# The second MLP product in three chunks: one group of 1024 output columns by seven products, in place of two groups of 512

## The chip, the cores and the metric

The kernel runs on one core of a Trainium2 chip. The metric is the device time of one launch in microseconds (us). TensorE (PE) multiplies into PSUM, which holds eight banks of 128 x 512 numbers; VectorE (DVE), ScalarE (ACT) and GpSimd (POOL) work on tiles; SyncE (SP) issues most DMAs. The engines run side by side, each through its own queue, and wait for one another by semaphores.

## The reference, cut to what matters

A decoder layer on 512 tokens of width 1024: two token mixers, a merge, and an MLP with a hidden width of 4096. The change is in the last product of the MLP.

```python
x = x + merged @ w_out[l]
h = rms_norm(x, norm_mlp[l])
x = x + jnp.square(jax.nn.relu(h @ w_ff1[l])) @ w_ff2[l]
return rms_norm(x, norm_final)
```

`h` is 512 x 1024, `w_ff1` 1024 x 4096, `w_ff2` 4096 x 1024, all float32.

## The kernel before, in words

**Precision.** A float32 operand is split into a high half (ACT copies it with rounding) and a low half (DVE subtracts: the line `DVE.tensor_tensor(l, t, h.bitcast(F32), op=ALU.subtract)`, L309). A product of two split operands is three matmuls: high by high, high by low, low by high. So each step of 128 in depth is three matmuls on PE, and every weight costs one ACT and one DVE instruction before PE can use it.

**The MLP** runs in four chunks `c` of 1024 hidden columns. In each, the first product gives the chunk's activations and the second adds their share to the output. Both are done by a scheme of seven products on 2 x 2 blocks in place of eight: the seven weight operands are three quarters of the weight block (A11, A12, A22) and four sums (S1 to S4), the seven activation operands are three blocks (y11, y21, y22) and four sums (yT1 to yT4). S1 = A21 + A22 and S3 = A11 + A21 are made in DRAM by DMAs (SP copies a quarter, POOL adds another, `make_sum` and `add_sum`); S2 = S3 + A22 and S4 = S2 + A12 are made in SBUF by DVE from weights that are there already (L318, and L297 where A12 is loaded a second time).

**The second product before the change** (`Out`, chunks 0 to 2) works in two groups `h` of 512 output columns. Each group's quarters of the weights are 512 rows by 256 columns. A product is 24 matmuls of 256 columns (L1520): the activations are stationary, the weights stream, two halves `f` of 128 tokens go to the two halves of one PSUM bank. Seven products in two groups are 14 x 24 = 336 matmuls per chunk. `OUT_TURN` gives the order; the first entry of a name is group 0, the second group 1. Three products add to a bank that an earlier one has left: A12 to A11's, S4 to S1's, A22 to S3's (`AFTER`). Before that the earlier product must have been **taken**: DVE adds the bank to the output `XX` (L1540, rows `x<-x,psB`) or, for A11 and S2, to a sum `U` that is kept through the chunks (L1536, rows `MA<-MA,psB`; in chunk 0 A11 is copied there by ACT, L1534). At the end `fold` adds `U` to three quarters of the output (L1546): group 1 after chunk 2, group 0 after chunk 3.

**Chunk 3** (`LAST`) does columns 0 to 511 by an `Out` of its own (`head`) and columns 512 to 1023 by plain matmuls of 512 columns (L395), in between.

**Weights.** Five buffers `raw` take loads from DRAM in the order of use; a buffer is loaded again as soon as its weights are split, or, where they go into a sum (`SUM_OF`), when that sum has been made (`give_back`). Three pairs of slots (`wh`/`wl` twice, `w3h`/`w3l`) hold the split weights; a slot is filled anew when PE has left the product that used it. In the orders below the pairs are `wh_4960`/`wl_4961`, `wh_4979`/`wl_4980` and `w3h`/`w3l`.

**What sets the order.** The program writes matmuls, and between them it lets the preparation of weights (`ahead`) and the side work (`step_side`: takes, activations, their sums and splits) go on by steps. A scheduler then orders each engine's instructions, and may put a later one ahead of one that it expects to wait. Each engine runs its queue in that order.

Of the kernel before, what the change touches and what calls it, by code (L numbers as in the profile page):

```python
# [13 lines left out]
F32 = mybir.dt.float32  # L14
FR = mybir.dt.float32r
AF = mybir.ActivationFunctionType
ALU = mybir.AluOpType
# [45 lines left out]
def trunk(ctx: ExitStack, tc: tile.TileContext, A, out):  # L63
    nc = tc.nc
    PE, ACT, DVE, POOL = nc.tensor, nc.scalar, nc.vector, nc.gpsimd
# [71 lines left out]
    LAST = 3  # L137
    FIRST = ("A11", "A12"), ("S1", "S3", "S2"), ("A22", "S4")
    IN_TURN = ("A11", "S3", "S1", "S2", "A12", "A22", "S4")
    OUT_TURN = ("A11", "A11", "S1", "S1", "A12", "A12", "S3", "S3", "A22", "A22", "S2", "S4", "S2", "S4")  # L140
    LAST_TURN = ("A11", "S1", "A12"), ("S3", "A22", "S2", "S4")
    dp = ctx.enter_context(tc.tile_pool(name="sums", bufs=1, space=bass.MemoryType.DRAM))
    jobs, late = [], []

    def quarters(layer, c, g):

        w, r, o = ((w_f1, 0, 1024 * c + 512 * g), (w_f2, 1024 * c, 512 * g))[layer - 1]
        return {f"{i + 1}{j + 1}": w[r + 512 * j:r + 512 * j + 512, o + 256 * i:o + 256 * i + 256].rearrange(
            "(k p) c -> p k c", p=128) for i in range(2) for j in range(2)}

    def add_group(layer, c, g):

        q = quarters(layer, c, g)
        of = {"A" + k: v for k, v in q.items()}
        final = layer == 2 and c == LAST
        for o in ("S1", "S3", "S2", "S4")[:4 if final else 4 - layer]:
            of[o] = dp.tile([128, 4, 256], F32, name=f"{o}_{layer}{c}{g}")
        jobs.append((of["S1"], q["21"], q["22"]))
        jobs.append((of["S3"], q["11"], q["21"]))
        if late:  # L160
            jobs.append(late.pop())
        if layer == 1:
            late.append((of["S2"], of["S1"], q["11"]))
        if final:
            jobs.append((of["S2"], of["S3"], q["22"]))
            jobs.append((of["S4"], of["S2"], q["12"]))
        return of
# [19 lines left out]
    for c in range(4):  # L187
# [7 lines left out]
        if c < LAST:  # L195
            of = [add_group(2, c, g) for g in range(2)]
            seen = {}
# [92 lines left out]
    def group_steps(i):  # L290

        key, at = WL[i]
        if i in PLUS:
            while st["load"] <= PLUS[i]:
                assert emit_load()
            t = raws.pop(PLUS[i])[0]
            DVE.tensor_tensor(t, t, held[key], op=ALU.add)  # L297
            give_back(held.pop(key))
            yield
        elif isinstance(at, str):  # L300
            t = held.pop(key)
        else:
            while st["load"] <= at:
                assert emit_load()
            t = raws.pop(at)[0]
        h, l = slot_of(i)
        ACT.activation(h, t, AF.Copy)  # L307
        yield
        DVE.tensor_tensor(l, t, h.bitcast(F32), op=ALU.subtract)  # L309
        hls[i] = tuple(x.rearrange("p (a b) -> p a b", a=4) for x in (h, l))  # L310
        to = SUM_OF.get(key)
        if to is None:
            give_back(t)
        elif to not in held:
            held[to] = t
        else:
            yield
            DVE.tensor_tensor(t, t, held[to], op=ALU.add)  # L318
            give_back(held[to])
            held[to] = t  # L320
# [62 lines left out]
    def use(key):  # L383
        i = st["use"]
        st["use"] += 1
        assert WL[i][0] == key, (WL[i][0], key)
        while st["prep"] <= i:
            emit_prep_half()
        return hls.pop(i)
# [21 lines left out]
    def step_side():  # L411
        for _ in range(len(side)):
            g = side.popleft()
            try:
                next(g)
                side.append(g)
            except StopIteration:
                pass
# [794 lines left out]
    def bank():  # L1213
        return ps3.tile([128, S], F32, tag="B", bufs=8, name="psB")
# [143 lines left out]
    def pair(f, i):  # L1358
        return f[:, 512 * i:512 * i + 512]
# [18 lines left out]
    def until(ready):  # L1378
        while not ready():
            assert side  # L1380
            step_side()

    class Group:
# [3 lines left out]
        def __init__(self, c, g, Y):  # L1387
            self.c, self.g, self.Y = c, g, Y
            self.s = pair(GBf, 6 + g)
            self.u2, self.u3, self.c21 = pair(MAf, 6 + g), pair(MAf, 0), pair(MAf, 1)  # L1390
            self.ps, self.done = {}, set()

        def pe(self, o):
            key = f"{o}1{self.c}{self.g}"
            until(lambda: o not in self.NEEDS or self.NEEDS[o] in self.done)
            if not self.done:
                side.append(self.main())
            name, x, *at = self.X[o]

            def mm(out, w, f, k, u, v, **kw):  # L1400
                PE.matmul(out, w[u][:, k, 128 * f:128 * f + 128], XB[x][v][:, k, :], **kw)  # L1401
            if not at:
                self.ps[name] = bank()
            product(self.ps[name], key, not at, mm)
            if at:
                side.append(self.last(name, *at))
            self.done.add(o)
# [95 lines left out]
    class Out:  # L1503
# [25 lines left out]

        def take(self, o, ps):  # L1530
            yield
            if o in ("A11", "S2"):
                if o == "A11" and self.c == 0:
                    ACT.activation(self.U, ps, AF.Copy)  # L1534
                else:
                    DVE.tensor_tensor(self.U, self.U, ps, op=ALU.add if o == "A11" else ALU.subtract)  # L1536
            else:
                i, j = {"A12": (0, 0), "S4": (0, 1), "A22": (1, 0)}.get(o, (1, 1))
                x = self.quarter(i, j)
                DVE.tensor_tensor(x, x, ps.rearrange("p (t c) -> p t c", t=2), op=ALU.subtract if i else ALU.add)  # L1540
            self.done.add(o)
# [6 lines left out]
                yield  # L1548
                yield

    def in_turn(groups, turn):

        seen = {}
        for o in turn:
            n = seen.get(o, 0)
            seen[o] = n + 1
            groups[n].pe(o)

    mode["pool"] = False
    for c in range(4):  # L1560
        Y = Hidden(c == LAST)
        gs = [Group(c, g, Y) for g in range(2)]
        if c == 0:
            for o in FIRST[0]:
                for g in gs:
                    g.pe(o)
            while not turned[0]:
                step_side()
            for os in FIRST[1:]:
                for g in gs:  # L1570
                    for o in os:
                        g.pe(o)
        else:
            for g in gs:
                for o in IN_TURN:
                    g.pe(o)
        if c < LAST:
            outs = [Out(c, h, Y) for h in range(2)]
            in_turn(outs, OUT_TURN)
            if c == LAST - 1:  # L1580
                side.append(outs[1].fold())

    def out_of(t):
        return MA[:, 2 * t:2 * t + 2, :].rearrange("p j c -> p (j c)")
# [22 lines left out]

    head = Out(LAST, 0, Y)
    keep([f"f2{LAST}1{i}" for i in range(4)], OT)
    in_turn([head], LAST_TURN[0])  # L1610
    w = []
    ps = [bank() for _ in range(2)]
    for i in range(4):
# [5 lines left out]
    for t in range(2):  # L1619
        add_x(t, 1, ps[t])  # L1620
        square_sum(t, 1)
    in_turn([head], LAST_TURN[1])
    gB = GBf[:, 0:D]
    nc.sync.dma_start(gB, bcast(A["norm_final"], D))
    while head.done != set(head.X):
# [48 lines left out]
```

## Time and profile before

| | us |
|---|---|
| median of 3 runs (812.71 to 813.44) | 813.04 |
| profiled execution, device time | 817.64 |
| its span | 815.9 |
| PE busy | 789.4 (97%) |
| DVE busy | 613.5 (75%) |
| ACT busy | 483.8 (59%) |
| POOL busy | 188.9 (23%) |
| second product, chunk 0, 1, 2 (first matmul to the next chunk's first) | 42.59, 41.12, 41.09 |
| first product, chunk 1, 2 | 39.94, 39.93 |

A row of the timeline gives the start, the duration, the engine, the line, what is written from what, the shapes, and in brackets how long the engine was idle before and what ended that. Matmuls overlap: the pace is the distance between starts, not the duration. Times within the span count from its start. L numbers are lines of the kernel before.

### The profile page before, as it was taken

What the parts mean: (1) busy time and instruction counts of PE and PEld (TensorE: products, weight loads), DVE (VectorE), ACT (ScalarE), POOL (GpSimd) and SP (SyncE); (2) the same over time, 40 slices, a digit from 0 to 9 for tenths busy, and PEclk for the clock granted to TensorE, in tenths of its full rate; (3) what the DMA queues carried; (4) which work ended last, traced back from release to release, by engine and by line L of the source; (5) the groups of instructions that cost most, each with busy time, mean ns of one, the idle gap of its engine ahead of it and who ended that gap; (6) DMA issues with size and microseconds to landing.
All of it is one profiled execution on the core that took longest, in us unless ns stands there. A gap on an engine that the chain in (4) does not pass through costs nothing.

```text
span 815.9 us, 14127 instructions
## 1 busy us (share of the span) xinstructions
PE 789.4 (97%) x5163; PEld 711.4 (87%) x5163; DVE 613.5 (75%) x1152; ACT 483.8 (59%) x957; POOL 188.9 (23%) x253
## 2 busy tenths in 40 slices
PE   8999989999998999999999999999999999999997
PEld 6888868788887888888788899999999999999996
DVE  5786744445987788889565578996889688978975
ACT  6765432325886788888334576844674467437833
POOL 4000000015775466665334100101010110000000
PEclk9999999999999999999999999999999999999999
DMA  9463752576965264335964717999998998654522
GB/s 291 136 177 92 193 152 71 152 187 171 199 124 121 59 123 106 78 78 120 317 156 147 199 17 199 313 235 284 257 273 221 280 262 213 204 178 156 174 85 104
DMA packets 131312, 140.84 MB, mean 173 GB/s; under 512 B 5862, under 2 KB 117514, under 8 KB 131083
## 3 DMA queue, kind: packets, MB, share of 16 engines
q1 hardware_dynamic: 109834, 118.18, 45.8%
q0 software_dynamic: 21120, 20.97, 18.3%
q8 instruction: 41, 0.67, 0.3%
q10 hardware_dynamic: 288, 0.79, 0.3%
q14 instruction: 29, 0.23, 0.1%
HBM read 131.01 MB, written 44.04 MB: 215 GB/s over the span
## 4 chain that ended last, share of the span: by engine, by line
PE 59%; DVE 14%; ACT 6%; issue 3%; DMA 3%; POOL 1%; SPq 0%; ACTq 0%; DVEq 0%; POOLq 0%
PE psF L395 16%; PE psB L395 12%; PE psB L1401 12%; PE psB L1520 9%; PE psO L1132 3%; PE psS L1030 3%; PE psT L1098 3%; DVE wl L309 3%; DMA Q<-rs 2%; DMA raw<-w_ff 1%; ACT P L1065 1%; DVE w3l L309 1%; DVE PT L1113 1%; ACT PT L1109 1%; ACT wh L307 1%
## 5 line engine op out<-in xcount | busy, mean ns | idle before, releaser
L395 PE MATMUL psF<-R,wh 128*128 128x512 f32 x512 | 168.0, 406 | 3.4 <-DVE yd L853 2.0
L307 ACT ACTIVATE wh<-raw 128x1024 fp32r<-128x1024 f32 x70 | 74.0, 1057 | 73.9 <-PE psB L1520 33.4
L274 POOL DMA_DIRECT2D S<-w_ff x40 | 46.3, 1157 | 297.3 <-DMA S<-w_ff 226.0
L395 PEld LDWEIGHTS psF<-R,wh 128*128 128x128 f32 x512 | 93.5, 190 | 22.4 <-DVE yd L853 2.4
L352 ACT ACTIVATE wh<-raw 128x512 fp32r<-128x512 f32 (+1 forms) x100 | 59.8, 619 | 77.2 <-PE psF L395 50.3
L395 PE MATMUL psF<-R,wl 128*128 128x512 f32 x256 | 102.0, 398 | 0.0
L309 DVE TENSOR_TENSOR wl<-raw,wh 128x1024 fp32r<-128x1024 f32 x70 | 85.2, 1218 | 17.9 <-ACT wh L307 17.9
L1081 POOL TENSOR_SCALAR P<-P,sm,GT 128x128 f32<-128x128 f32 (+3 forms) x128 | 80.7, 665 | 58.2 <-DVE sm L1071 47.4
L354 DVE TENSOR_TENSOR wl<-raw,wh 128x512 fp32r<-128x512 f32 (+1 forms) x74 | 52.9, 723 | 35.2 <-ACT wh L352 34.6
L1065 ACT ACTIVATE P<-P,sm 128x128 f32<-128x128 f32 (+3 forms) x128 | 71.1, 557 | 9.8 <-DVE sm L1055 8.9
L1055 DVE CUSTOM_DVE_ANT_0 P<-psS,cst 128x128 f32<-128x128 f32 (+3 forms) x128 | 59.7, 483 | 14.3 <-PE psT L1098 6.2
L1401 PE MATMUL psB<-R,wh 128*128 128x256 f32 x352 | 64.1, 282 | 0.0
L1113 DVE TENSOR_TENSOR PT<-psT,PT 128x512 fp32r<-128x512 f32 (+2 forms) x96 | 56.4, 596 | 7.5 <-ACT PT L1109 6.8
L307 ACT ACTIVATE w3h<-raw 128x1024 fp32r<-128x1024 f32 x35 | 37.0, 1056 | 39.5 <-PE psB L1520 17.1
L395 PEld LDWEIGHTS psF<-R,wl 128*128 128x128 f32 x256 | 48.6, 190 | 11.1
L1109 ACT ACTIVATE PT<-psT 128x512 fp32r<-128x512 f32 (+2 forms) x96 | 49.2, 520 | 13.7 <-PE psT L1098 12.6
L1098 PE MATMUL psT<-ident,P 128*128 128x128 f32 x320 | 50.5, 274 | 5.0 <-ACT pc L1001 4.3
L1401 PEld LDWEIGHTS psB<-R,wh 128*128 128x128 f32 x352 | 54.2, 188 | 0.3 <-DVE R L1343 0.2
L309 DVE TENSOR_TENSOR w3l<-raw,w3h 128x1024 fp32r<-128x1024 f32 x35 | 42.7, 1219 | 14.9 <-ACT w3h L307 14.9
L1098 PEld LDWEIGHTS psT<-ident,P 128*128 128x128 f32 x320 | 39.4, 141 | 13.9 <-issue 6.9
L1401 PE MATMUL psB<-R,wl 128*128 128x256 f32 x176 | 49.5, 281 | 0.0
L1132 PE MATMUL psO<-PT,VV 128*128 128x256 f32 x320 | 49.0, 290 | 0.0
(387 smaller groups left out, 2253.0 us busy)
## 6 DMA issues: line engine op xcount, KB each, us to landing
raw<-w_ff SPq DMA_DIRECT2D x55, 512.0 KB, 5.0
S<-w_ff POOLq DMA_DIRECT2D x40, 512.0 KB, 7.7
raw<-S SPq DMA_DIRECT2D x40, 512.0 KB, 5.1
raw<-w_in SPq DMA_DIRECT2D x32, 512.0 KB, 4.3
S<-w_ff SPq DMA_DIRECT2D x30, 512.0 KB, 5.9
S<-S SPq DMA_DIRECT2D x10, 512.0 KB, 7.0
raw<-w_proj_nsa SPq DMA_DIRECT2D x8, 512.0 KB, 4.1
raw<-w_out SPq DMA_DIRECT2D x8, 512.0 KB, 3.5
```

Of the source, the lines that this page charges most:

```text
L307: ACT.activation(h, t, AF.Copy)
L309: DVE.tensor_tensor(l, t, h.bitcast(F32), op=ALU.subtract)
L352: ACT.activation(h[:, sl], t[:, sl], AF.Copy)
L395: PE.matmul(ps, a, b, start=first and j == 0, stop=last and j == n - 1, skip_group_check=True)
L1055: DVE.tensor_tensor_reduce(out=P[:, o:o + n].rearrange("p (a c) -> p a c", c=128), in0=s, in1=m, scale=1.0, scalar=3e38, op0=ALU.add, op1= ...
L1065: last_exp[:] = [ACT.activation(c, c, AF.Exp, bias=sm[:, 0, e:e + 1], scale=-1.0, accum_out=sm[:, 1, e:e + 1])]
L1081: r = POOL.tensor_scalar(P[:, o:o + n], P[:, o:o + n], sm[:, 2, e:e + 1], GT[:, qb, c + e:c + e + 1], op0=ALU.mult, op1=ALU.mult)
L1098: PE.transpose(pt[:, 128 * j:128 * j + 128], P[:, 128 * j:128 * j + 128], ident)
L1113: DVE.tensor_tensor(dL, src, dH.bitcast(F32), op=ALU.subtract)
L1132: PE.matmul(ps[:, qb % 2, :, :], VV[:, k, b, g, :], t[:, j, :, :], start=False, stop=last and j == len(kbs) - 1 and t is tL, skip_group_ch ...
L1401: PE.matmul(out, w[u][:, k, 128 * f:128 * f + 128], XB[x][v][:, k, :], **kw)
L1520: PE.matmul(out, YB[y][u][:, k, 128 * f:128 * f + 128], w[v][:, k, :], **kw)
```

## The change

In chunks 0 to 2 the two `Out` groups become one `Wide`. A quarter is now 512 x 512, and comes in two parts of 256 rows by 512 columns, so that a part still fills one slot and one load. A matmul streams 512 columns, one half `f` of the tokens goes to one bank, and a name in `OUT_TURN` stands for one part of the depth: part 0 uses the first 256 hidden columns of the activations, part 1 the rest. The 336 matmuls of 256 columns per chunk become 168 of 512. A product is taken when both parts are done, by two instructions of 512 columns where there were two of 2 x 256. S3 and A12 go by turns. `U` is folded for all columns after chunk 2 (six instructions in place of three), so the last chunk's A11 is copied to `U` by ACT.

```diff
-    OUT_TURN = ("A11", "A11", "S1", "S1", "A12", "A12", "S3", "S3", "A22", "A22", "S2", "S4", "S2", "S4")
+    OUT_TURN = ("A11", "A11", "S1", "S1", "S3", "A12", "S3", "A12", "A22", "A22", "S2", "S4", "S2", "S4")
...
     def quarters(layer, c, g):
 
+        if layer == 2 and c < LAST:
+            return {f"{i + 1}{j + 1}": w_f2[1024 * c + 512 * j + 256 * g:1024 * c + 512 * j + 256 * g + 256,
+                                            512 * i:512 * i + 512].rearrange("(k p) c -> p k c", p=128)
+                    for i in range(2) for j in range(2)}
...
-            of[o] = dp.tile([128, 4, 256], F32, name=f"{o}_{layer}{c}{g}")
+            of[o] = dp.tile(list(q["11"].shape), F32, name=f"{o}_{layer}{c}{g}")
...
         def take(self, o, ps):
             yield
-            if o in ("A11", "S2"):
-                if o == "A11" and self.c == 0:
-                    ACT.activation(self.U, ps, AF.Copy)
-                else:
-                    DVE.tensor_tensor(self.U, self.U, ps, op=ALU.add if o == "A11" else ALU.subtract)
+            if o == "A11":
+                ACT.activation(self.U, ps, AF.Copy)
+            elif o == "S2":
+                DVE.tensor_tensor(self.U, self.U, ps, op=ALU.subtract)
...
+    class Wide:
...
+        def pe(self, o):
+            name, y = self.X[o]
+            part = self.seen.get(o, 0)
+            self.seen[o] = part + 1
+            fresh = o not in self.AFTER
+            if part == 0:
+                until(lambda: self.Y.ready(y) and (fresh or self.AFTER[o] in self.done))
+                if fresh:
+                    self.ps[name] = [bank() for _ in range(2)]
+            w, n = use(f"{o}2{self.c}{part}"), 0
+            for f in range(2):
+                for k in range(2):
+                    for u, v in ((0, 0), (0, 1), (1, 0)):
+                        PE.matmul(self.ps[name][f], YB[y][u][:, 2 * part + k, 128 * f:128 * f + 128], w[v][:, k, :],
+                                  start=fresh and part == 0 and k == u == v == 0, stop=part == 1 and k == 1 and u == 1,
+                                  skip_group_check=True)
+                        n += 1
+                        if n % 3 == 0:
+                            ahead()
+                            step_side()
+            if part == 1:
+                side.append(self.take(o, self.ps[name]))
...
-            outs = [Out(c, h, Y) for h in range(2)]
-            in_turn(outs, OUT_TURN)
+            wide = Wide(c, Y)
+            for o in OUT_TURN:
+                wide.pe(o)
             if c == LAST - 1:
-                side.append(outs[1].fold())
+                side.append(wide.fold())
```

How this moves instructions, at the places that the prediction speaks of (a row is the line, the operation, what is written from what, and its shape; lines of the changed kernel are its own).

PE, chunk 0, where A12 (y21) and S3 (yT3) meet, before: the end of A12's group 0, one matmul of S3, then A12's group 1.

```order
L1520 MATMUL psB<-wh_4960,y21H 128x256
L1520 MATMUL psB<-wl_4961,y21H 128x256
L1520 MATMUL psB<-wh_4960,y21L 128x256
L1520 MATMUL psB<-w3h,yT3H 128x256
L1520 MATMUL psB<-wl_4980,y21H 128x256
L1520 MATMUL psB<-wh_4979,y21L 128x256
L1520 MATMUL psB<-wh_4979,y21H 128x256
```

PE at the same place in the changed kernel, from the end of S1: S3's part 0 uses `wh_4960`/`wl_4961`, A12's part 0 `wh_4979`/`wl_4980`, S3's part 1 `w3h`/`w3l`.

```order
L1578 MATMUL psB<-wh_4960,yT3H 128x512 x2
L1578 MATMUL psB<-wh_4979,y21H 128x512 x2
L1578 MATMUL psB<-wl_4961,yT3H 128x512 x2
L1578 MATMUL psB<-wh_4960,yT3L 128x512
L1578 MATMUL psB<-wh_4960,yT3H 128x512
L1578 MATMUL psB<-wl_4961,yT3H 128x512
L1578 MATMUL psB<-wh_4960,yT3L 128x512 x2
L1578 MATMUL psB<-wh_4960,yT3H 128x512
L1578 MATMUL psB<-wl_4961,yT3H 128x512
L1578 MATMUL psB<-wh_4960,yT3L 128x512
L1578 MATMUL psB<-w3h,yT3H 128x512 x2
L1578 MATMUL psB<-wl_4980,y21H 128x512
```

S3 has moved ahead of A12, and of each part the two matmuls that need only high halves stand ahead of the first that needs a low half of the part before.

DVE, chunk 0, from the last split before the takes of the second product, before: takes (`x_4536<-x_4536,psB`, in the order S1, S1, A12, A12, S3) alternate with splits (`wl`, `w3l`) and the sums of weights for S2 (`raw`).

```order
L309 TENSOR_TENSOR wl_4980<-raw_4950,wh_4979 128x1024
L1540 TENSOR_TENSOR x_4536<-x_4536,psB 128x2x256
L309 TENSOR_TENSOR w3l<-raw_4547,w3h 128x1024
L1540 TENSOR_TENSOR x_4536<-x_4536,psB 128x2x256
L309 TENSOR_TENSOR wl_4961<-raw_4912,wh_4960 128x1024
L1540 TENSOR_TENSOR x_4536<-x_4536,psB 128x2x256
L309 TENSOR_TENSOR wl_4980<-raw_4890,wh_4979 128x1024
L1540 TENSOR_TENSOR x_4536<-x_4536,psB 128x2x256
L318 TENSOR_TENSOR raw_4890<-raw_4890,raw_4547 128x1024
L309 TENSOR_TENSOR w3l<-raw_4938,w3h 128x1024
L1540 TENSOR_TENSOR x_4536<-x_4536,psB 128x2x256
```

DVE at the same place in the changed kernel; the takes are S1 (two), S3's first half, S3's second half.

```order
L313 TENSOR_TENSOR wl_4980<-raw_4950,wh_4979 128x1024
L313 TENSOR_TENSOR w3l<-raw_4547,w3h 128x1024
L1599 TENSOR_TENSOR x_4536<-x_4536,psB 128x512 x2
L313 TENSOR_TENSOR wl_4961<-raw_4912,wh_4960 128x1024
L313 TENSOR_TENSOR wl_4980<-raw_4890,wh_4979 128x1024
L1599 TENSOR_TENSOR x_4536<-x_4536,psB 128x512
L323 TENSOR_TENSOR raw_4890<-raw_4890,raw_4938 128x1024
L313 TENSOR_TENSOR w3l<-raw_4950,w3h 128x1024
L1599 TENSOR_TENSOR x_4536<-x_4536,psB 128x512
```

S3 is taken ahead of A12, its first half ahead of the sum and the split that stood before S3's take.

ACT, chunk 3, before: `R_63` is the high half of the weights for the plain matmuls, `MA<-MA` an activation of the first product.

```order
L1457 ACTIVATE yT2H<-MA 128x512
L352 ACTIVATE R_63<-raw_4890 128x512
L352 ACTIVATE R_63<-raw_4547 128x512 x2
L352 ACTIVATE R_63<-raw_4950 128x512
L1467 ACTIVATE MA<-MA 128x512
```

ACT at the same place in the changed kernel.

```order
L1462 ACTIVATE yT2H<-MA 128x512
L357 ACTIVATE R_63<-raw_4890 128x512
L357 ACTIVATE R_63<-raw_4938 128x512 x2
L1538 ACTIVATE MA<-psB 128x512
L1472 ACTIVATE MA<-MA 128x512
```

The copy of A11 (L1538) has come in behind three of the four `R_63` rows, and the row of DVE that added A11 to `U` is gone.

More of the change, by code (lines that the diff above doesn't have):

```diff
@@ L309, in group_steps @@
         DVE.tensor_tensor(l, t, h.bitcast(F32), op=ALU.subtract)
-        hls[i] = tuple(x.rearrange("p (a b) -> p a b", a=4) for x in (h, l))
+        a = 2 if key[-3] == "2" and int(key[-2]) < LAST else 4
+        hls[i] = tuple(x.rearrange("p (a b) -> p a b", a=a) for x in (h, l))
         to = SUM_OF.get(key)
@@ L1549, in fold, with __init__, take @@
                 yield
[L1551 to L1557, printed above, removed]
+    class Wide:
+        def __init__(self, c, Y):
+            self.c, self.Y = c, Y
+            self.U = [pair(MAf, 4 + f) for f in range(2)]
+            self.ps, self.done, self.seen = {}, set(), {}
+        X, AFTER = Out.X, Out.AFTER
+        def pe(self, o):
[20 more added lines that the diff above has]
+                side.append(self.take(o, self.ps[name]))
+        def take(self, o, ps):
+            yield
+            for f in range(2):
+                if o in ("A11", "S2"):
+                    if o == "A11" and self.c == 0:
+                        ACT.activation(self.U[f], ps[f], AF.Copy)
+                    else:
+                        DVE.tensor_tensor(self.U[f], self.U[f], ps[f], op=ALU.add if o == "A11" else ALU.subtract)
+                else:
+                    i, j = {"A12": (0, 0), "S4": (0, 1), "A22": (1, 0)}.get(o, (1, 1))
+                    x = XX[:, 2 * j + f, 512 * i:512 * i + 512]
+                    DVE.tensor_tensor(x, x, ps[f], op=ALU.subtract if i else ALU.add)
+            self.done.add(o)
+        def fold(self):
+            for f in range(2):
+                for i, j in ((0, 1), (1, 0), (1, 1)):
+                    x = XX[:, 2 * j + f, 512 * i:512 * i + 512]
+                    DVE.tensor_tensor(x, x, self.U[f], op=ALU.subtract if i else ALU.add)
+                    yield
+                    yield
+                    yield
@@ L1609, in trunk @@
     keep([f"f2{LAST}1{i}" for i in range(4)], OT)
-    in_turn([head], LAST_TURN[0])
+    for o in LAST_TURN[0]:
+        head.pe(o)
     w = []
@@ L1621, in trunk @@
         square_sum(t, 1)
-    in_turn([head], LAST_TURN[1])
+    for o in LAST_TURN[1]:
+        head.pe(o)
     gB = GBf[:, 0:D]
```

## The prediction

> **What bounds the kernel now.** I read the page first. TensorE (PE) is busy 97% of the span at full granted clock, so a shorter time must come out of PE's own rows: a faster pace or fewer waits.
>
> ```profile
> span 815.9 us, 14127 instructions
> PE 789.4 (97%) x5163; PEld 711.4 (87%) x5163; DVE 613.5 (75%) x1152; ACT 483.8 (59%) x957; POOL 188.9 (23%) x253
> ```
>
> This execution took 817.64 us with 1.7 us outside the span; the plain runs have a median of 813.04. I work out a saving in the trace and take it off the median.
>
> Then the busy time by stretches: from the first matmul of the second product (L1520) in chunks 0, 1 and 2 to the first of the next chunk's L1401, with the first product of chunks 1 and 2 between them.
>
> ```profile
> core 0: us, PE busy (x) PEld busy (x) DVE busy (x) ACT busy (x) POOL busy (x), PEclk, DMA share, GB/s
> 521.04:563.63 42.59, 41.00 (x338) 40.22 (x337) 39.44 (x48) 23.07 (x30) 4.66 (x5) 1.00 1.00 268
> 563.63:603.57 39.94, 39.94 (x338) 39.94 (x337) 30.66 (x35) 25.50 (x36) 4.62 (x4) 1.00 0.98 264
> 603.57:644.69 41.12, 40.48 (x339) 40.10 (x337) 37.95 (x46) 20.71 (x26) 4.65 (x4) 1.00 0.95 250
> 684.62:725.71 41.09, 40.48 (x339) 40.10 (x337) 38.65 (x48) 20.70 (x26) 1.16 (x1) 1.00 0.68 195
> ```
>
> Both products have 336 matmuls of 256 columns per chunk. The first runs without a gap; the second takes 1.2 to 2.6 us longer, and there DVE is nearly full (39.44 of 42.59). So the second product is bound by PE, with waits for DVE. These are its waits, and one in the last chunk:
>
> ```profile
> 530.32 0.38 PE L1520 MATMUL psB<-w3l,yT1H 128*128 128x256 f32 x1 [0.44 <-DVE w3l L309]
> 530.54 0.28 PE L1520 MATMUL psB<-w3h,yT1L 128*128 128x256 f32 x1
> 533.87 0.39 PE L1520 MATMUL psB<-wl,y21H 128*128 128x256 f32 x1 [0.30 <-DVE wl L309]
> 537.41 0.39 PE L1520 MATMUL psB<-wl,y21H 128*128 128x256 f32 x1 [0.42 <-DVE wl L309]
> 546.41 0.36 PE L1520 MATMUL psB<-wh,yT4H 128*128 128x256 f32 x1 [0.43 <-DVE x L1540]
> 618.44 0.39 PE L1520 MATMUL psB<-w3l,y21H 128*128 128x256 f32 x1 [0.20 <-DVE w3l L309]
> 627.47 0.36 PE L1520 MATMUL psB<-w3h,yT4H 128*128 128x256 f32 x1 [0.44 <-DVE x L1540]
> 699.50 0.39 PE L1520 MATMUL psB<-wl,y21H 128*128 128x256 f32 x1 [0.20 <-DVE wl L309]
> 708.52 0.36 PE L1520 MATMUL psB<-wh,yT4H 128*128 128x256 f32 x1 [0.42 <-DVE x L1540]
> 775.12 0.39 PE L1520 MATMUL psB<-wh,y21H 128*128 128x256 f32 x1 [0.45 <-DVE MA L1536]
> ```
>
> Two kinds stand here: a low half of a weight that DVE has not split yet (wl, w3l), and a take (x, MA) that must empty a bank before the next product adds to it. A wait costs about 0.1 to 0.2 us more than its idle time shows, since ends are modelled, and 0.1 on restarting (530.32 to 530.54, where 0.12 is the pace).
>
> **The pace.** Pure stretches give it from start to start.
>
> ```profile
> 521.04 0.28 PE L1520 MATMUL psB<-w3h,y11H 128*128 128x256 f32 x1
> 529.60 0.28 PE L1520 MATMUL psB<-w3h,yT1H 128*128 128x256 f32 x1
> 798.29 0.62 PE L395 MATMUL psB<-R,xT2H 128*128 128x512 f32 x2
> 803.88 0.40 PE L395 MATMUL psB<-R,xT2H 128*128 128x256 f32 x2
> ```
>
> Between the first two lie 72 matmuls of 256 columns: 8.56 / 72 = 0.119 us. Between the last two lie 24 of 512, with activations stationary and weights streaming as in the new product: 5.59 / 24 = 0.233 us. The change replaces 3 x 336 of the first by 3 x 168 of the second: 39.98 - 39.2 (at 0.2333) = 0.79 us per chunk, **2.4 us** in all. What the stages of before lasted beyond 39.98 is their waits: 2.6, 1.14 and 1.11 us. Bounds: at 0.235, just above the row, 504 x 0.003 = 1.5; at 0.2305, just below, 504 x 0.0075 = 3.8. I take the row itself, since its operands lie the same way.
>
> The Trainium skill, "TensorE: Matmul & The Clock Gate", section "Wait — 56ns, not 53.3ns?", has warm matmuls start N / 2.4 GHz plus a fixed 2.5 ns apart. By it halving their number is worth an estimated 504 x 2.5 ns = 1.3 us and the whole sum below would be 5.2 instead of 6.3. The trace's paces (119 and 233, where the rule has 109 and 216) are both slower than it, by unequal amounts, so the rows decide.
>
> **The waits, chunk 0.** Products go by A11, S1, then S3 and A12 by turns, then A22, S2, S4; (0) and (1) are a product's two parts. Before, S3's take stood in DVE's queue behind a sum of weights (L318) and a split:
>
> ```profile
> 536.14 1.21 DVE L309 TENSOR_TENSOR wl<-raw,wh 128x1024 fp32r<-128x1024 f32 x1
> 537.27 0.68 DVE L1540 TENSOR_TENSOR x<-x,psB 128x512 f32<-128x512 f32 x1
> 543.32 1.22 DVE L318 TENSOR_TENSOR raw<-raw,raw 128x1024 f32<-128x1024 f32 x1
> 544.45 1.22 DVE L309 TENSOR_TENSOR w3l<-raw,w3h 128x1024 fp32r<-128x1024 f32 x1
> 545.59 0.68 DVE L1540 TENSOR_TENSOR x<-x,psB 128x512 f32<-128x512 f32 x1
> 542.98 0.28 PE L1520 MATMUL psB<-wh,yT3H 128*128 128x256 f32 x1
> 543.23 1.06 ACT L307 ACTIVATE w3h<-raw 128x1024 fp32r<-128x1024 f32 x1 [1.68 <-PE psB L1520]
> ```
>
> From one row to the next a split or sum takes 1.14 and a take 0.6; ACT fills a slot 0.25 us after PE has left it (at 542.98 for the next product). I go through the new order with these. A11 and S1 are 48 matmuls: 521.04 + 11.2 = 532.24; S1(1)'s low half stands one 0.6 us row earlier on DVE than it did, so PE gets it at about 529.7, when it wants it. Four matmuls that need only high halves follow, to 533.2; then S3(0) needs the split that came at 533.87, and DVE has the same work ahead of it: a wait of 0.7. Twelve matmuls later, at 536.8 (0.1 lost on restarting), A12(0) needs the one of 537.41: a wait of 0.6. Then 32 matmuls and 0.1 bring PE to A22 at 544.98, where it stood at 546.41. Is S3 taken by then? DVE's new order after the split of 536.14: split to 538.4, two takes of S1 to 539.6, split to 540.75, A22(0)'s split (its high half, 1.06 on ACT, can begin when A12(0) ends, 539.84 + 0.25) to 542.3, S3's first half taken by 542.9, sum to 544.05, split to 545.2, second half taken by 545.8. PE wants the halves at 544.98 and 546.38. So the waits at the take go, with 0.6 us to spare. After that 72 matmuls: 561.8 instead of 563.63, **1.85 us**, of which 0.8 is pace. A wait for the split of S4(0), which now stands behind S2(1)'s, is covered: PE has four matmuls of S2(1) ahead of the ones that need it.
>
> **Chunks 1 and 2.** The first matmul that needs A12(0)'s low half is the 65th: 603.57 + 64 x 0.2333 = 618.5, and 684.62 + 14.93 = 699.55. PE got that split at 618.44 and 699.50, behind the same work. No wait is left, and the take comes as in chunk 0. Both stages would last 39.2 instead of 41.12 and 41.09: **1.9 us** each. Bounds for the waits of the three chunks: all stay (0) or all go (4.9); I take 1.05 + 1.14 + 1.11 = 3.3.
>
> **The last chunk.** A11 is now fresh: a copy on ACT (L1534 before, where c is 0) in place of DVE's sum MA, which DVE reached at 774.39 although S1 had followed A11 at 769.07.
>
> ```profile
> 769.07 0.28 PE L1520 MATMUL psB<-wh,yT1H 128*128 128x256 f32 x1
> 774.39 0.67 DVE L1536 TENSOR_TENSOR MA<-MA,psB 128x512 f32<-128x512 f32 x1
> 769.86 2.18 ACT L352 ACTIVATE R<-raw 128x512 fp32r<-128x512 f32 x4
> 771.94 0.62 ACT L1467 ACTIVATE MA<-MA 128x512 f32<-128x512 f32 x1
> ```
>
> The copy stands behind three of these four R rows: 769.86 + 3 x 0.52 = 771.4, done at 771.9. PE, which has the 11 L395 matmuls now behind A12, wants it when S1 ends, at 769.07 + 24 x 0.119 = 771.93. The gap ahead of 775.12 (0.6 over the pace) goes: **0.6 us**; bounds 0 and 0.7.
>
> **Edits at nothing.** Three more folds (0.6 each) on DVE in chunk 3's first product: the stretch at 563.63 shows 9.3 us of DVE idle in such a stage, and a split has 3.4 us of cover there (ready 2.3 us after its slot is free, wanted two products of 2.85 later); without cover 1.8. Loads in 2 KB instead of 1 KB rows:
>
> ```profile
> raw<-w_ff SPq DMA_DIRECT2D x55, 512.0 KB, 5.0
> raw<-S SPq DMA_DIRECT2D x40, 512.0 KB, 5.1
> raw<-w_out SPq DMA_DIRECT2D x8, 512.0 KB, 3.5
> ```
>
> Rows of 1 KB and 4 KB land alike here (5.0, 5.1), and w_out's of 2 KB in 3.5: between nothing and 1 us gained, I take nothing. GpSimd adds 12 of its sums in half as many rows; POOL is busy 188.9 us of 815.9, and I take nothing there either.
>
> **Sum:** 2.4 + 3.3 + 0.6 = 6.3 us: 813.04 - 6.3 = **806.7**. From 813.04, 0.2% (1.6 us) is about what a measurement tells from no change.
>
> **Rivals.** *The waits stay.* DVE is the fuller engine: with the stage at 39.2 its 38 to 39 us leave almost nothing idle, and the fit of 618.44 against 618.5 has no slack. Then a faster PE meets the next split instead, and only the pace is left: 810.6. For: DVE has 39.44 us of work in the 42.59 of chunk 0. Against: in chunks 1 and 2 it idles 2.4 to 3.2 us, and the order puts its takes and splits where the steps above need them.
>
> *Late loads (slower).* S3(0)'s weights are held through A12(0), so the buffer for A22(1) comes free one product later: its load starts when A12(0)'s split ends, at 537.4, and ACT wants it at 542.4.
>
> ```profile
> 537.41 0.37 SPq L236 DMA_DIRECT2D raw<-w_ff  x1
> DMA to landing us min/median/max: 5.0/5.0/5.0
> 618.45 0.37 SPq L236 DMA_DIRECT2D raw<-w_ff  x1
> DMA to landing us min/median/max: 3.5/3.5/3.5
> DMA to landing us min/median/max: 3.8/5.2/8.3
> ```
>
> The load of 537.41 landed in 5.0, that of 618.45 in 3.5; over 520 to 565 the range is 3.8 to 8.3. With 0.6 us of slack behind DVE, 6.1 us does no harm; each us above costs 1 us per chunk through S3's second take, which queues behind that split. It cancels the gain at 8.2 us in all three chunks, and is slower by over 1.6 at 8.7; at 9.5 the time is 813.04 - 6.3 + 3 x 3.4 = 816.9. Only the slowest landing speaks for it.
>
> *The change does not do what it says:* 512 columns of split weights run at twice 0.119, and as many waits come up elsewhere: 813. The L395 rows speak against it.
>
> **How the numbers follow.** Forecast 0.66, waits stay 0.20, no effect 0.08, late loads 0.06. Faster takes the forecast and most of the second: 0.83; same 0.11; slower 0.06. The range goes from 804.6 (pace at its upper bound and 0.7 more of the waits gone) to 810.9, just past the case where only the pace is left.
>
> **What would show it.** Right: 504 matmuls of 512 columns at 0.233; the three stages at about 40.7, 39.2 and 39.2 us; no PE wait for x at A22; in chunk 0 two waits for wl of some 0.7; A12 of the last chunk close on S1. Wrong: stages near 40.3 or longer with PE waiting for wl or w3l (waits stay), ACT waiting for the DMA of raw ahead of A22(1) (late loads), or a pace above 0.236.

## The result, and the profile after

The changed kernel takes **807.27 us** (median of 6 runs, 806.98 to 810.94); the kernel before has 813.96 in the 6 runs beside it. The ratio is 0.9926, with a 95% interval of 0.9904 to 0.9948: faster by 0.5 to 1.0%. One slow execution of 2717.48 us, in the run of the turns alone, is left out of that run's ratio and stands in its median. The profiled execution took 810.94 against 817.64, 6.70 us less, and its span is 6.7 shorter. Two lines of its page:

```profile
span 809.2 us, 13118 instructions
PE 785.0 (97%) x4659; PEld 685.3 (85%) x4659; DVE 613.1 (76%) x1154; ACT 484.1 (60%) x958; POOL 188.3 (23%) x253
```

PE has 504 matmuls fewer and is busy 4.4 us less; the span shrank by more, so waits went too. DVE does the same work as before. By stretches of the changed kernel, with the columns of the prediction's table: the second product (now L1578) in chunks 0, 1 and 2, from its first matmul to the next chunk's first L1406, and in the second row the first product of chunk 1.

```profile
521.05:561.36 40.31, 39.56 (x171) 31.23 (x169) 37.94 (x47) 22.19 (x29) 3.71 (x4) 1.00 0.93 255
561.36:601.30 39.94, 39.94 (x337) 39.94 (x336) 30.91 (x36) 25.50 (x36) 5.12 (x5) 1.00 0.99 281
601.30:640.40 39.10, 39.10 (x170) 31.39 (x169) 37.33 (x46) 20.65 (x26) 3.47 (x3) 1.00 0.94 247
680.31:719.38 39.07, 39.07 (x171) 31.40 (x169) 37.25 (x46) 20.66 (x26) 1.16 (x1) 1.00 0.67 194
```

The stages were 42.59, 41.12 and 41.09: they give 2.28, 2.02 and 2.02 us, 6.32 together. The first product is as long as before (39.94), and so is the stretch in which the folds moved (40.49 in chunk 3, before 40.50). The last chunk's second product gives the rest: from 759.87 to the start of the last matmul it lasts 42.93, before 43.31.

What is left of waits stands in chunk 0. The timeline of the changed kernel there, first PE, then DVE, then ACT:

```profile
533.09 0.74 PE L1578 MATMUL psB<-wl,yT3H 128*128 128x512 f32 x2
534.30 0.50 PE L1578 MATMUL psB<-wh,yT3L 128*128 128x512 f32 x1 [0.47 <-DVE yT3L L1465]
545.32 0.40 PE L1578 MATMUL psB<-wh,yT4L 128*128 128x512 f32 x1
546.00 0.50 PE L1578 MATMUL psB<-wh,yT4H 128*128 128x512 f32 x1 [0.28 <-DVE x L1599]
...
533.55 0.69 DVE L1465 TENSOR_TENSOR yT3L<-GB,yT3H 128x512 fp32r<-128x512 f32 x1
541.56 0.68 DVE L1599 TENSOR_TENSOR x<-x,psB 128x512 f32<-128x512 f32 x1
542.15 1.22 DVE L323 TENSOR_TENSOR raw<-raw,raw 128x1024 f32<-128x1024 f32 x1
544.12 1.23 DVE L313 TENSOR_TENSOR w3l<-raw,w3h 128x1024 fp32r<-128x1024 f32 x1 [0.75 <-ACT w3h L311]
545.26 0.68 DVE L1599 TENSOR_TENSOR x<-x,psB 128x512 f32<-128x512 f32 x1
...
543.03 1.06 ACT L311 ACTIVATE w3h<-raw 128x1024 fp32r<-128x1024 f32 x1 [2.65 <-DMA raw<-w_ff]
```

What a wait costs is the distance between two starts less the pace of 0.232, and the matmul after it loses another 0.1 on restarting. At 533.09 S3 waits for the split of its weights (0.2 with the restart), and at 534.30 for the low half of its *activations* (0.63, and 0.1 on restarting): 0.9 in all. At 546.00 A22's second half waits 0.45 for S3's second take: that take stands on DVE behind a split, the split behind ACT's high half, and that behind a load that was issued at 536.65 and was there at 543.03. In the last chunk, ACT's copy of A11 and PE's first matmul of A12:

```profile
763.62 1.66 ACT L357 ACTIVATE R<-raw 128x512 fp32r<-128x512 f32 x3
765.18 0.57 ACT L1538 ACTIVATE MA<-psB 128x512 f32<-128x512 f32 x1
...
765.81 0.39 PE L1525 MATMUL psB<-wh,y21H 128*128 128x256 f32 x1
```

The copy stands behind three R rows as forecast, and the gap ahead of A12 is 0.22 over the pace instead of 0.62.

### The profile page after: what moved, and what is told of

Same layout as the page of the kernel before. It is cut to its first block, busy times and chain, and to the rows that moved or that the text cites. A ratio compares the mean times of both kernels' runs of the same rounds, so it can differ in the third digit from the quotient of the medians.

```text
span 809.2 us, 13118 instructions
## 1 busy us (share of the span) xinstructions
PE 785.0 (97%) x4659; PEld 685.3 (85%) x4659; DVE 613.1 (76%) x1154; ACT 484.1 (60%) x958; POOL 188.3 (23%) x253
## 4 chain that ended last, share of the span: by engine, by line
PE 65%; DVE 7%; ACT 6%; DMA 4%; issue 2%; POOL 1%; SPq 0%; ACTq 0%; POOLq 0%; DVEq 0%
PE psB L1406 16%; PE psF L400 16%; PE psB L1578 12%; PE psB L400 10%; PE psO L1137 3%; PE psS L1035 3%; PE psT L1103 3%; PE psB L1525 2%; DMA Q<-rs 2%; DMA raw<-w_ff 1%; ACT P L1070 1%; DMA raw<-w_out 1%; DVE PT L1118 1%; ACT PT L1114 1%; PE psC L970 1%
## 5 line engine op out<-in xcount | busy, mean ns | idle before, releaser
L1406 PE MATMUL psB<-R,wh 128*128 128x256 f32 x352 | 64.1, 282 | 0.0
L1406 PEld LDWEIGHTS psB<-R,wh 128*128 128x128 f32 x352 | 54.3, 189 | 0.5 <-DVE R L1348 0.2
L1406 PE MATMUL psB<-R,wl 128*128 128x256 f32 x176 | 49.5, 281 | 0.0
```

## The experiments

My theory after the result: the gain has two terms of like size, PE's pace in matmuls of 512 columns (about 1 us per chunk) and waits for DVE (about 1 us per chunk), and the waits go only because order and width work together. Rivals: the order alone, or the width alone, carries it; or loads in longer rows do.

The part ahead of the MLP differs by several us from one execution to the next (the first product of chunk 0 begins at 471.9 to 477.8 us in these traces), and single times scatter by as much, while a stage of chunk 1 or 2 repeats to 0.1 us where nothing in it was edited. Chunk 0 repeats less well: two traces of the old second product have 42.59 and 43.19 there, two of the changed kernel 40.31 and 40.56. So the verdicts rest on stages, those of chunks 1 and 2 first, with the times beside them.

**The old order in the wide group.**

```diff
-    OUT_TURN = ("A11", "A11", "S1", "S1", "S3", "A12", "S3", "A12", "A22", "A22", "S2", "S4", "S2", "S4")
+    OUT_TURN = ("A11", "A11", "S1", "S1", "A12", "A12", "S3", "S3", "A22", "A22", "S2", "S4", "S2", "S4")
```

> The changed kernel with the old order of products in chunks 0 to 2 (A12, A12, S3, S3 instead of S3, A12, S3, A12). Nothing of the computation changes. Theory (the turns keep S3's take out of PE's way): A22 now follows S3 at once, and S3's second half is taken behind a sum and a split; 0.25 + 0.6 + 1.14 + 0.6 = 2.6 us after PE leaves S3, where PE wants it after 1.4, so 1.0 to 1.3 us per chunk come back as a PE wait for x at L1599, three times: 810.3 to 811.2. The wait for yT3L in chunk 0 should go in return (A12 comes first there), so 809.5 to 810.4 in all. Rival (the gain is the matmuls' pace and DVE's general load, the order does not matter): 807.3, stages as in the changed kernel (40.3, 39.1, 39.1).

Measured: 812.68 us, 0.9979 [0.9964, 0.9994] of before. The stages are 41.64, 40.76 and 40.75: 1.33, 1.66 and 1.68 us given back, more than expected. PE and ACT in chunk 0, and PE in chunk 1:

```profile
541.99 0.73 PE L1578 MATMUL psB<-wh,yT2H 128*128 128x512 f32 x2 [1.20 <-ACT wh L311]
622.71 0.50 PE L1578 MATMUL psB<-wh,yT2H 128*128 128x512 f32 x1 [1.20 <-ACT wh L311]
...
540.88 1.06 ACT L311 ACTIVATE wh<-raw 128x1024 fp32r<-128x1024 f32 x1 [1.74 <-PE psB L1578]
```

The wait has the place and the size, but not the name: PE waits for S2's weights, not for x. The scheduler has put two matmuls of S2 ahead of A22, and their slot is the one that S3 had just left (0.25 + 1.06 on ACT). DVE's first take of S3 ends only at 542.2 here, so A22 could hardly have begun sooner. 0.3 more per chunk stand ahead of A12 in chunks 1 and 2. The wait in chunk 0 that should have gone in return came back as 0.90 for the split of A12. So the width without the turns keeps only 1.65 us of the three stages' 6.32.

**Only the last chunk's part, in the kernel before.**

```diff
-                if o == "A11" and self.c == 0:
+                if o == "A11" and self.c in (0, LAST):
...
-                side.append(outs[1].fold())
+                side.extend(o.fold() for o in outs)
```

> The kernel before with only the last chunk's part of the change: its A11 is copied by ACT, and both groups' sums are folded after chunk 2 (one fold of three rows moved there). Theory, from the two traces: the wait ahead of A12 in the last chunk shrinks from 0.62 to 0.22, and nothing else moves: 813.96 - 0.4 = 813.5. The prediction's own term: 0.6, 813.3. Rival (the three folds on DVE cost something in the last chunk's first product): no gain or a loss, 813.9 to 814.5. The difference is near what can be measured, so the trace decides: PE's start of A12 against S1 in the last chunk, and the length of the last chunk's first product (40.1 in both kernels).

Measured: 815.01 us, 0.9998 [0.9982, 1.0014]: no difference that the time shows. In the trace the first product of the last chunk is 40.49 again, so the folds cost nothing, and the second is 43.13. Its copy and the first matmul of A12:

```profile
768.65 0.58 ACT L1534 ACTIVATE MA<-psB 128x512 f32<-128x512 f32 x1
769.28 0.39 PE L1520 MATMUL psB<-wh,y21H 128*128 128x256 f32 x1 [0.26 <-ACT MA L1534]
```

The copy began 5.51 us after the product's first matmul (763.14); PE is there for A12 after 5.72. In the twelve traces with this copy the gap ahead of A12 lies between 0 and 0.73 over the pace, 0.3 in the mean, and it follows the moment at which ACT reaches the copy (5.22 us after the product's start in one, 5.82 in another; 4.86 to 6.25 over all). Without it, it was 0.62 and 0.66. The term exists and is about half of what I gave it.

**Only the turns, in the kernel before** (the same line of `OUT_TURN` as in the change).

> The kernel before, two groups and matmuls of 256 columns, with only the new order (S3 and A12 by turns). Nothing of the computation changes. Theory: S3's take of each group has a product more before A22, so the waits for x at A22 go (0.55 to 0.65 in each of three chunks), the waits for low halves stay or move by little: stages about 42.0, 40.5, 40.5, the time 813.96 - 1.8 = 812.2. If the turns carried all of the waits (3.3): 810.7. If they only help together with one group: 813.9.

Measured: 813.78 us, 0.9993 [0.9975, 1.0010], stages 41.82, 40.85, 40.87: 0.77, 0.27 and 0.22 us gained. The waits at A22 are gone in all three chunks, as expected, but a new one stands ahead of S3. PE in chunk 1, and the row of DVE that it waits for:

```profile
608.30 0.28 PE L1520 MATMUL psB<-wh,yT3H 128*128 128x256 f32 x1
608.53 0.28 PE L1520 MATMUL psB<-w3h,y21H 128*128 128x256 f32 x1
609.41 0.39 PE L1520 MATMUL psB<-wh,yT3L 128*128 128x256 f32 x1 [0.60 <-DVE yT3L L1460]
...
608.66 0.69 DVE L1460 TENSOR_TENSOR yT3L<-GB,yT3H 128x512 fp32r<-128x512 f32 x1
```

The changed kernel at the same place:

```profile
612.43 0.40 PE L1578 MATMUL psB<-wh,yT3H 128*128 128x512 f32 x1
613.37 0.63 PE L1578 MATMUL psB<-w3h,y21H 128*128 128x512 f32 x2
613.84 0.50 PE L1578 MATMUL psB<-wh,yT3L 128*128 128x512 f32 x1
...
613.09 0.69 DVE L1465 TENSOR_TENSOR yT3L<-GB,yT3H 128x512 fp32r<-128x512 f32 x1
```

DVE begins yT3L 11.8 us after the stage's start in both (608.66 - 596.87; 613.09 - 601.30). PE wants it 0.36 us after S3's first matmul in one (three matmuls of 256), 1.41 us after in the other (six of 512). So the turns bring S3 forward onto yT3L, and the width gives PE work that covers it. This is why the turns do little by themselves; the wide group in the old order loses 1.5 us per chunk ahead of A22 with the restart, as shown above. Turns alone give 1.26 us in the three stages, width alone 1.65, both 6.32; in chunks 1 and 2, which repeat, 0.49, 0.70 and 4.04.

**The pace alone**: the changed kernel with each matmul cut in two.

```diff
+                        for e in range(2):
+                            cs = slice(256 * e, 256 * e + 256)
+                            PE.matmul(self.ps[name][f][:, cs], YB[y][u][:, 2 * part + k, 128 * f:128 * f + 128],
+                                      w[v][:, k, cs], start=fresh and part == 0 and k == u == v == e == 0,
+                                      stop=part == 1 and k == 1 and u == 1 and e == 1, skip_group_check=True)
```

> The changed kernel with each matmul of 512 columns cut into two of 256 (same operands, same order, same takes; 336 instead of 168 per chunk). Theory: the pace goes back from 0.2323 to 2 x 0.119 = 0.238, 168 x 3 x 0.0057 = 2.9 us more on PE; the wait of 0.56 at A22 in chunk 0 is partly absorbed, since PE comes there later: 807.27 + 2.4 to 2.9 = 809.7 to 810.2; stages 40.9 to 41.2, 40.0, 40.0. By the rule of a fixed 2.5 ns for each matmul: 807.27 + 1.3 = 808.5, stages 39.5. Rival (the width of matmuls is not where the gain is): 807.3.

Measured: 811.61 us, 0.9962 [0.9942, 0.9982]. By stretches, chunks 0 to 2:

```profile
517.28:557.76 40.48, 40.44 (x338) 40.16 (x337) 38.13 (x47) 22.26 (x29) 3.46 (x4) 1.00 0.93 258
597.70:637.92 40.22, 40.22 (x338) 40.10 (x337) 37.41 (x46) 20.71 (x26) 4.62 (x4) 1.00 0.96 253
677.85:718.08 40.23, 40.23 (x338) 40.10 (x337) 37.85 (x47) 20.71 (x26) 1.16 (x1) 1.00 0.68 201
```

Chunks 1 and 2 are 1.12 and 1.16 longer than in the changed kernel, with nothing over 0.1 lost at a place in either: this is the pace by itself. Chunk 0 is only 0.17 longer, since a slower PE waits less there (0.4 ahead of S3, nothing at A22). So of the 6.32 us of the three stages 3.87 come with matmuls of 256 columns already, and 2.45 with those of 512. It also tells which part of the width covers yT3L: in chunk 1 PE has nine matmuls of 256 columns (1.1 us) between S3's first and the one that needs yT3L, where two groups in the same order had three. That is the wide group, not the length of a matmul. The rule in the Trainium skill, "TensorE: Matmul & The Clock Gate", section "Wait — 56ns, not 53.3ns?" (a fixed 2.5 ns for each matmul) gives an estimated 0.42 per chunk for 168 matmuls more; the measured 1.1 decides.

**Loads in two pieces of 1 KB rows.**

```diff
+    def half_rows(q):
+        if q.shape[2] == 512:
+            return [(q[:, :, 0:256], 0), (q[:, :, 256:512], 256)]
+        return [(q, 0)]
...
-            LD.append([(of[g][o], 0)])
+            LD.append(half_rows(of[g][o]))
```

> The changed kernel with each load of the second product's weights in chunks 0 to 2 split into two transfers of half the columns, so that rows are 1 KB again, as before the change (the sums in DRAM are left in 2 KB rows). Nothing of the computation changes. Theory (row length is worth nothing here): landings of raw stay at 5 us in the median, stages 40.3, 39.1, 39.1, the time 807.3 within 0.5. Rival (2 KB rows bring the loads earlier, and part of the gain is theirs): landings of 6 us or more, PE waits for splits behind them, 808 to 809.5.

Measured: 808.79 us, 0.9942 [0.9917, 0.9966]. Chunks 1 and 2 are as in the changed kernel (39.11 and 39.07); chunk 0 is 42.08. There, PE, DVE and ACT:

```profile
543.54 0.50 PE L1583 MATMUL psB<-wh,yT4H 128*128 128x512 f32 x1 [1.51 <-DVE x L1604]
...
541.66 1.23 DVE L318 TENSOR_TENSOR w3l<-raw,w3h 128x1024 fp32r<-128x1024 f32 x1 [2.00 <-ACT w3h L316]
...
540.57 1.06 ACT L316 ACTIVATE w3h<-raw 128x1024 fp32r<-128x1024 f32 x1 [3.90 <-DMA raw<-w_ff]
```

It is the chain of 546.00 again, with the load there 23.8 us after the stage's start instead of 22.0. The median landing of the pieces from `w_ff` stays at 5.2 us (of those from the sums it is 6.2), so one load decides here and not the median. **The same kernel once more:**

> The run with 1 KB rows once more, nothing else edited, one look. If the late landing in chunk 0 comes from the load being issued in two pieces: stage near 42 again, the wait at A22 near 1.7. If it was chance: 40 to 41.

Measured: 810.58 us in one execution; stages 41.81, 39.74, 39.08, with 1.81 lost at A22 in chunk 0 (and 0.51 in chunk 1). The load that decides came late both times, and again in the last run below, so chance is an unlikely account. Its two pieces, issued 0.41 us apart, land one after the other: the first 3.6 and 2.8 us after its issue in the two traces, the second 7.1 and 7.2 after its own. Whether the row length or the two issues delay the load is not told apart: before the change rows of 1 KB came in one transfer.

**Four buffers for loads instead of five.**

```diff
-    give_back(p4.tile([128, 1024], F32, name="raw5"))
```

> The changed kernel with four buffers for loads instead of five in the MLP. Nothing of the computation changes. It prices the rival of late loads: a load starts when a buffer comes free, so with one buffer fewer each starts about one product (2.85 us) later. Theory (in chunk 0 the load of A22's second part already lands with no slack, and S3's second take queues behind its split): 2 to 2.85 us more in chunk 0, 1 to 2.8 more in each of chunks 1 and 2, where the load lands earlier than it is wanted: 811 to 816. Rival (loads have slack, and the chunk-0 wait has another cause): 807.3 to 808.

Measured: 816.27 us, 1.0022 [1.0006, 1.0039], slower than the kernel before. Stages 41.91, 40.46 and 40.82: 1.60, 1.36 and 1.75 more than in the changed kernel (in chunk 0 less than expected), and another 4.2 in chunk 0's first product. In chunk 2 PE meets the split itself. DVE came to it late, since ACT had waited for this load and for the one before it:

```profile
712.33 0.50 PE L1577 MATMUL psB<-wl,yT4H 128*128 128x512 f32 x1 [1.01 <-DVE wl L313]
...
706.98 1.23 DVE L313 TENSOR_TENSOR wl<-raw,wh 128x1024 fp32r<-128x1024 f32 x1 [2.05 <-ACT wh L311]
...
705.89 1.06 ACT L311 ACTIVATE wh<-raw 128x1024 fp32r<-128x1024 f32 x1 [4.44 <-DMA raw<-w_ff]
708.36 1.06 ACT L311 ACTIVATE wh<-raw 128x1024 fp32r<-128x1024 f32 x1 [1.41 <-DMA raw<-w_ff]
```

So the late loads of the prediction's rival are a real mechanism; with five buffers and loads in one piece they reach PE in chunk 0 alone.

**The takes one step earlier.**

```diff
         def take(self, o, ps):
-            yield
             for f in range(2):
...
             self.done.add(o)
+            yield
```

> The changed kernel with each take handed to the scheduler one step earlier (the generator's first pause is moved to its end), which puts the second half of S3's take ahead of A22's second split on DVE, in chunk 0 too. Nothing of the computation changes. Theory (the wait of 0.56 at A22 in chunk 0 is that take queued behind the split, which waits for a load): the wait goes, the stage is 39.7 instead of 40.3, the time 806.7. Rival (the take is late for another reason, or another row of DVE is late next): stage 40.3, 807.3, or a wait for w3l of A22's second part of up to 0.5 in its place.

Measured: 807.61 us, 0.9927 [0.9901, 0.9952]; stage 40.20, the others 39.07 and 39.06. DVE now takes S3's second half ahead of the split, and PE's wait at A22 is gone:

```profile
537.65 0.68 DVE L1598 TENSOR_TENSOR x<-x,psB 128x512 f32<-128x512 f32 x1
538.25 1.22 DVE L323 TENSOR_TENSOR raw<-raw,raw 128x1024 f32<-128x1024 f32 x1
539.39 0.68 DVE L1598 TENSOR_TENSOR x<-x,psB 128x512 f32<-128x512 f32 x1
539.98 1.22 DVE L313 TENSOR_TENSOR w3l<-raw,w3h 128x1024 fp32r<-128x1024 f32 x1
...
529.20 0.72 PE L1578 MATMUL psB<-wl,yT3H 128*128 128x512 f32 x2 [0.30 <-DVE wl L313]
530.40 0.50 PE L1578 MATMUL psB<-wh,yT3L 128*128 128x512 f32 x1 [0.48 <-DVE yT3L L1465]
```

The stage gains only 0.1, because the waits ahead of S3 are longer in this execution (1.3 with the restarts, 0.9 before): DVE reached the same rows 0.4 us later, counted from the stage's start. By an estimate from these rows the take in its old place would have ended here about when PE wanted it, so this run shows that the order changed, and not yet what that is worth.

**The same, and chunk 0 in the order A12, S3, S3, A12.**

```diff
+    TURN0 = ("A11", "A11", "S1", "S1", "A12", "S3", "S3", "A12", "A22", "A22", "S2", "S4", "S2", "S4")
...
-            for o in OUT_TURN:
+            for o in (OUT_TURN if c else TURN0):
```

> As the run before it, and chunk 0 alone in the order A12, S3, S3, A12, so that yT3 is needed one product later; S3 still has a whole product before A22. Nothing of the computation changes. Theory (the wait of 0.84 in chunk 0 is for yT3L, the low half of the activations, and not for a split of weights): both waits of chunk 0 go, stage 39.1 to 39.3 as in the other chunks, the time 807.27 - 0.56 - 0.84 = 805.9. Rival (the first wait is DVE's backlog as a whole and comes up again at the next row): stage 39.7, 806.6.

Measured: 807.06 us, 0.9926 [0.9904, 0.9948], stage 40.55: missed. The wait for yT3L is gone, but the scheduler put the first matmul of A12's second part ahead of most of S3, and its slot had just been left by A12's first part:

```profile
532.26 0.50 PE L1579 MATMUL psB<-wh,y21H 128*128 128x512 f32 x1 [1.15 <-ACT wh L312]
...
531.15 1.06 ACT L312 ACTIVATE wh<-raw 128x1024 fp32r<-128x1024 f32 x1 [1.41 <-PE psB L1579]
```

**The changed kernel again, unedited.**

> The changed kernel once more, nothing edited, for the scatter that one execution has. Both theories: stages of chunks 1 and 2 within 0.1 of 39.10 and 39.07. In chunk 0 theory (DVE's backlog at the start of the stage and the landing of one load set its waits, and both vary): 40.0 to 41.2 with the same two places of waiting; rival (chunk 0 is as fixed as the others, and the 42.1 of the run with 1 KB rows is all due to the rows): 40.3 within 0.1. The time: 807.3 within 1.

Measured: 808.27 us, 0.9908 [0.9892, 0.9924]; stages 40.56, 39.06, 39.06. Chunk 0 lost 0.2 ahead of S1's second split, 1.4 ahead of S3 (0.65 for the split of its weights, 0.74 for yT3L), and nothing at A22, where ACT began on the load 21.35 us after the stage's start. Its waits vary from one execution to the next; those of the other chunks don't.

**yT3 before the rows for T2 and T4**, with the takes first.

```diff
             DVE.tensor_tensor(f12, f22, f12, op=ALU.subtract)
             yield
-            DVE.tensor_tensor(f22, f22, f11, op=ALU.add)
-            yield
             side.append(self.split("T3", f, f12))
+            while not self.ready("T3"):
+                yield
+            DVE.tensor_tensor(f22, f22, f11, op=ALU.add)
+            yield
```

> The run with the takes first, and in the making of the activations the sums for T2 and T4 are held until both halves of T3 are split, in all four chunks; so that DVE makes yT3L three rows (1.8 us) or more earlier. Nothing of the computation changes. Theory (chunk 0's first wait is DVE's row order: rows for A22 and S2 stand ahead of the one that S3 waits for): that wait of 0.84 to 1.3 shrinks to 0.3 or less, the one at A22 stays away, stage 39.1 to 39.6, the others unchanged at 39.1: 807.3 - 1.0 = 806.3. Rival (DVE has as much work up to A22 in any order, and the wait comes back at A12's or A22's splits): 40.2, 807.

Measured: **806.07 us**, 0.9883 [0.9865, 0.9901] of before, the shortest of all. By stretches:

```profile
518.36:557.65 39.29, 39.15 (x171) 31.48 (x170) 37.73 (x47) 22.20 (x29) 3.36 (x3) 1.00 0.98 263
597.59:636.54 38.95, 38.95 (x171) 31.57 (x169) 37.18 (x46) 20.53 (x26) 3.47 (x3) 1.00 0.95 248
676.46:715.35 38.89, 38.89 (x170) 31.56 (x169) 37.14 (x46) 20.66 (x26) 1.16 (x1) 1.00 0.67 190
```

117.13 us for the three stages, against 118.48 and 118.68 in the two traces of the changed kernel. In chunk 0 only 0.4 is lost, for the split of S3's second part; yT3L starts 9.45 us after the stage's start (527.81 in its trace) instead of 12.50. Chunks 1 and 2 lost their last restart too, by 0.1 to 0.2, which was not expected. It beats the kernel before; that it beats the changed kernel rests on the stages of this one execution, while the intervals of the two ratios overlap.

**1 KB rows with the takes first** (the edits of those two runs together).

> The run with 1 KB rows together with the takes first. Nothing of the computation changes. Theory (a load that lands late costs time through S3's second take, which stood behind that load's split): with the take ahead of the split the 1.8 us at A22 in chunk 0 go, but for up to 0.5 at A22's second part, which needs the split itself: stage 40.2 to 40.8, the time 807.3 to 808. Rival (the loads in two pieces cost time by themselves, at PE's or ACT's own need): stage near 42.

Measured: 808.23 us, 0.9915 [0.9897, 0.9933], stage 40.82 instead of 42.08 and 41.81. Nothing is lost at A22, 0.9 ahead of S3, and three splits of S2 and S4 come late by 0.2 to 0.45. DVE there:

```profile
540.61 0.68 DVE L1603 TENSOR_TENSOR x<-x,psB 128x512 f32<-128x512 f32 x1
542.83 1.23 DVE L318 TENSOR_TENSOR w3l<-raw,w3h 128x1024 fp32r<-128x1024 f32 x1 [1.55 <-ACT w3h L316]
```

The load is as late as in the two runs before (ACT begins on it 23.33 us after the stage's start; 23.76 and 23.49), and the take no longer stands behind it: S3's second take was the way by which it reached A22. It was not its whole price, for DVE still idles 1.55 us for that load, and 1.06 comes back at the splits of S2 and S4.

## Why the prediction was right, and where not

The forecast was 806.7 and the median is 807.27. The traces differ by 6.7 us and the medians of the same measurement (813.96 and 807.27) by as much, where the sum was 6.3; the forecast still lies below, because its base was the 813.04 of three earlier runs. By its steps:

- **The pace, 2.4: too small, 2.9 to 3.4.** Chunks 1 and 2 run 168 matmuls in 39.0 us without their one restart: 0.232, where I had taken 0.2333 from the L395 rows; that makes 0.98 per chunk against 39.98. Cutting the matmuls in two costs 1.12 to 1.16. It lies inside my bounds of 1.5 and 3.8. Net of the waits that the faster PE then meets in chunk 0 it is 2.45.
- **The waits of chunks 1 and 2, 1.14 and 1.11: right.** 0.1 is left in each, on restarting. What I had not seen is that yT3L comes with no slack there: the order alone runs into it.
- **Chunk 0, 1.85 with pace: 2.28, for other reasons.** The first stop has about its size (0.8 forecast with the restart, 0.9 here), but other parts: 0.2 for the split of S3's weights, and 0.7 for yT3L, which DVE makes two rows behind that split and which my steps did not have. In the second trace of the changed kernel the split costs 0.65, as I had it, and yT3L another 0.74. The wait of 0.6 at A12 is in neither trace: here A12's split began at 535.36, before at 536.14; in the other it began as late as before, and PE came later by its wait for yT3L. So PE came to A22 0.8 us sooner here than I had it, and wanted the second half at 545.55 instead of 546.38. **"So the waits at the take go, with 0.6 us to spare" is the step that failed:** my own time for that take (545.8) was met within 0.15, and PE was early. DVE would have been early too, but it idled 0.75 us for the high half behind the load. The runs with 1 KB rows, without the takes first (1.8 lost at A22) and with them (nothing, with the load as late), show that the take's place behind that split made this wait. One wait that I had not seen (yT3L), one that did not come (A12) and one that I had called gone (A22) nearly cancel: it is partly luck that the stage came out near its forecast (40.31 and 40.56 against 40.7).
- **The last chunk, 0.6: too large.** The gap shrank by 0.4 here and by 0.3 in the mean of the traces, since ACT reaches the copy at a time that varies by over 1 us.
- **Edits at nothing.** The folds: nothing, shown twice (40.49). The rows of the loads: nothing in chunks 1 and 2; in chunk 0, two transfers of 1 KB rows lose 1.3 to 1.8 against the two traces of the changed kernel, so there was something to lose, and I can't say how much of it belongs to the rows.
- **The rivals.** That the waits stay holds with the old order (0.9979). Late loads show in the changed kernel's chunk 0 alone, at about 0.5 us in one trace and none in the other. In the first ACT began on the load at 543.03, earlier than the 543.5 that I had called harmless (537.4 + 6.1), and it still cost that, because PE wanted the take sooner. One buffer fewer brings late loads into all three stages and makes the kernel slower than before. At a landing of 8.7 us my rule gives a loss of 1.5 us, and not over 1.6 as I wrote. No effect is excluded by the interval.

Open: why the load in two pieces lands later, and what moves DVE's rows in chunk 0 by up to 0.8 us between executions, counted from the stage's start (yT3L begins at 12.50 and 13.29 in the two traces of the changed kernel).

## What to carry to other kernels

When PE is full and another engine nearly so, a new order moves a wait to the next row that was just in time: before counting a wait as gone, write down for each later operand when PE will now want it and when its engine makes it, activations as well as weights. Two edits that gain a fifth and a quarter of the whole by themselves (in chunks 1 and 2 an eighth and a sixth) can gain all of it together, when one opens a wait that the other covers. And a consumer's take should not stand in a queue behind work that waits for a transfer.

## What the runs showed of the hardware

A matmul of 512 columns with new stationary data each time takes 0.232 us from start to start, two of 256 take 0.238. With 256 columns the weight loads fill the stage (40.10 of 40.22 us in the run of the pace alone), with 512 they take 31.4 of 39.1; that this sets the difference was not tried. The matmul after one that has waited starts 0.1 us late as well (534.30 to 534.63 in the changed kernel's chunk 0, where the pace is 0.232). A load of 512 KB was there 6.4 us after its issue in the changed kernel's chunk 0, although the median of such loads is 5.3, and that one landing held the split and the take that PE waited for.
